# Two heads' recurrent state in fixed block-diagonal tiles: a decoder step's delta-rule scan on one core

## The chip, the cores and the metric

The kernel runs on one core of a Trainium2 chip, as one program. The metric is the device time of an execution in microseconds; a time is given as the median of several runs. A core has a matrix engine (TensorE; PE in the profile, with PEld for its loads of the stationary operand), a vector engine (VectorE, DVE), a scalar engine (ScalarE, ACT), GpSimd (POOL), and queues for transfers (here all issued by SP). Each engine works through its own instructions in order; semaphores join them. Products land in PSUM, from which DVE and ACT read.

## The reference

One step of a decoder layer over 1024 prompt tokens and 8 samples of 8 tokens: a Mamba-2 branch, an RWKV-7 branch, a merge and a gated convolutional feed-forward part. The change lies in the RWKV-7 branch alone, whose core is a recurrence over time for each of 16 heads with a state S of 64 x 64:

```python
def step(S, inp):
    r_t, w_t, k_t, v_t, kk_t, a_t = inp
    sa = jnp.einsum('bhvk,bhk->bhv', S, -kk_t)
    S = (S * w_t[:, :, None, :] + sa[..., None] * (kk_t * a_t)[:, :, None, :]
         + v_t[..., None] * k_t[:, :, None, :])
    return S, jnp.einsum('bhvk,bhk->bhv', S, r_t)
```

The prompt starts with S = 0; the samples start with given states. Decay, keys, rates and gates come from projections of the normalized input, and a group norm, a bonus and a gate follow. All results are fp32.

## The kernel before

The kernel keeps activations with channels on the 128 partitions and tokens along the free dimension, in three groups of tokens, `tg` = 0, 1, 2, with 384, 384 and 320 tokens (the last 64 are the samples'). Dense products are made with an fp32r value split in a high and a low part, three products for each (`mm3`, L254 to L257), from weights split on the way (`split_w`, L237 and L238).

The recurrence runs by chunks. Two heads share the partitions: one pair `p` of eight has head 0 on partitions 0 to 63 and head 1 on 64 to 127. A chunk, or unit `u`, is 64 steps; `tg` 0 and 1 have six units of the prompt, `tg` 2 four of them and one unit for the samples. For each pair and token group four jobs follow one another: `rw_prep` (decays, keys, masks, L486), `rw_inv` (inverse of the unit's triangular system, L601), `rw_scan` (the sequential part, L752) and `rw_post` (norm and gate, L865). Each is a generator in a lane of its own; `run_dense` takes a step of each lane (`bg.step()`) after every second inner block of six dense products, so that these small jobs stand between the dense products in PE's queue. The final order of the instructions on an engine is settled at build time by the framework's scheduler, from its planned costs and from which operands are ready; it need not be the order in which the program issues them. In the first third of the kernel all this runs; the Mamba-2 branch, the merge and the feed-forward part follow.

`rw_scan` goes like this for each unit. The state `st` is a tile of 128 x 128 in a rotating pool of eight buffers; head 0 occupies its upper left quadrant, head 1 its lower right one. L771 multiplies it with the unit's keys `ar[:, u, 0:2]` (128x128), DVE adds `rv` (L773), L775 multiplies with the inverse, DVE and ACT copy the two diagonal quadrants to `sav` (L776, L777), L779 multiplies with the decayed keys, and L781 makes the next state from all 128 x 128 elements: the old one times the unit's decay `wend`, plus the product in PSUM. The off-diagonal quadrants of the state are not used; what they give in L771 falls out later, as the quadrants of `tt` beside the diagonal are zero.

After the units of a token group come their outputs in `py` (L785 to L792), as two terms: the state at the start of the unit times the unit's `ar[:, u, 2]` (`own`), and `sav` times a masked product `tt`. Both are made by quadrant: `own` has a 64x64 stationary operand for each head, the other term a 128x64 one. `small` (L241) makes them follow one another in PE's queue, after the last product of the units. ACT and DVE then split `py` in a high and a low part (`halves`, L397) for the group norm's products.

For `tg` 0 a fresh state is filled with zeros by POOL (L758); after `tg` 2 the two quadrants of the last state are stored.

Of the kernel before, what the change touches and what calls it, by code (L numbers as in the profile page):

```python
# [10 lines left out]
F32 = mybir.dt.float32  # L11
F32R = mybir.dt.float32r
AF = mybir.ActivationFunctionType
ALU = mybir.AluOpType
# [90 lines left out]
def tile_hybrid_step(  # L105
# [6 lines left out]
    V, S, G, PE = nc.vector, nc.scalar, nc.gpsimd, nc.tensor  # L112
# [16 lines left out]
    def pst(shape=(128, 512)):  # L129
        return pp.tile(list(shape), F32, tag="t", name="pst", bufs=PB[1])  # L130
# [21 lines left out]
    def cv(name):  # L152
        o, w = CON[name]
        return con[:, o:o + w]
# [86 lines left out]
    def small(calls, behind=None, wait=None):  # L241

        for call in calls:
            if behind is None:
                behind = call().ins
            else:
                with tc.issue_after(behind):
                    behind = call().ins
            if wait is not None:
                tc.add_manual_dep(behind, wait.name, mybir.DependencyInfo(mybir.DependencyClass.Sync, mybir.DependencyReason.DATA), reason="small")  # L250
                wait = None
# [47 lines left out]
    def store(dst, src):  # L299
        nc.sync.dma_start(dst, src)  # L300
# [3 lines left out]
    rp = rw_stack.enter_context(tc.tile_pool(name="rp", bufs=1))  # L304
# [14 lines left out]
    for t in ars:  # L319
        G.memset(t[64:128, :, 0, :], 0.0)  # L320
        G.memset(t[0:64, :, 1, :], 0.0)

    llo = rp.tile([128, 2, 128], F32R, name="llo")
    G.memset(llo[64:128, 0, :].bitcast(F32), 0.0)
# [2 lines left out]
    def rt(shape, tag, bufs=1, dt=F32):  # L327
        return rp.tile(list(shape), dt, tag=tag, name=tag, bufs=bufs)
# [58 lines left out]
    start = Background({"norm": first})  # L387
# [9 lines left out]
    def halves(src, n):  # L397

        xh, xl = rt([128, 384], "xh", dt=F32R), rt([128, 384], "xl", dt=F32R)
        S.copy(xh[:, :n], src[:, :n])  # L400
        V.tensor_tensor(out=xl[:, :n], in0=src[:, :n], in1=xh[:, :n].bitcast(F32), op=ALU.subtract)
        return xh, xl
# [349 lines left out]
    def rw_scan(p, tg):  # L752
        t0, n = TG[tg]
        npu = 6 if tg < 2 else 4
        ar, tt, sav, bkt, wend, rv = jobs.pop((p, tg))
        if tg == 0:
            st = rt([128, 128], "st", 8)
            G.memset(st, 0.0)  # L758
            state[p] = st
        if tg == 2:  # L760
            s0 = rt([128, 8, 64], "s0", 1)
            nc.sync.dma_start(s0, rw0[p])
        yt = rt([128, 384], "yt", 2)

        two = lambda t: t.rearrange("p (h c) -> p h c", h=2)
        sts = []
        for u in range(npu):
            st = state[p]
            sts.append(st)
            pc = pp.tile([128, 3, 128], F32, tag="c", name="pc", bufs=2)  # L770
            PE.matmul(pc[:, 0, :], ar[:, u, 0:2, :].rearrange("p h c -> p (h c)"), st, start=True, stop=True)  # L771
            rh = rt([128, 128], "rh", 2)
            V.tensor_tensor(out=two(rh), in0=two(pc[:, 0, :]), in1=rv[:, u, :].unsqueeze(1).to_broadcast([128, 2, 64]), op=ALU.add)  # L773
            yield
            PE.matmul(pc[:, 1, :], tt[:, u, 0:2, :].rearrange("p h c -> p (h c)"), rh, start=True, stop=True)  # L775
            V.tensor_copy(sav[0:64, u, 0, :], pc[0:64, 1, 0:64])  # L776
            S.copy(sav[64:128, u, 1, :], pc[64:128, 1, 64:128])  # L777
            yield
            last = PE.matmul(pc[:, 2, :], bkt[:, u, :], sav[:, u, :, :].rearrange("p h c -> p (h c)"), start=True, stop=True).ins  # L779
            st2 = rt([128, 128], "st", 8)  # L780
            V.scalar_tensor_tensor(out=st2, in0=st, scalar=wend[:, u:u + 1], in1=pc[:, 2, :], op0=ALU.mult, op1=ALU.add)  # L781
            state[p] = st2
            yield

        py = pp.tile([128, 384], F32, tag="y", name="py", bufs=1)  # L785

        def out(u, hf, own):
            r = slice(64 * hf, 64 * hf + 64)
            lhs, rhs = (sts[u][r, r], ar[r, u, 2, :]) if own else (sav[:, u, hf, :], tt[:, u, 2 + hf, :])
            return PE.matmul(py[r, 64 * u:64 * u + 64], lhs, rhs, start=own and u == 0, stop=not own and u == npu - 1, skip_group_check=True)  # L790

        small([lambda u=u, hf=hf, own=own: out(u, hf, own) for own in (True, False) for u in range(npu) for hf in range(2)], last)  # L792
        del sts
        yield
        if tg == 2:
            S.copy(yt[:, :npu * 64], py[:, :npu * 64])
            for r in (slice(0, 64), slice(64, 128)):
                store(rw_p_o[p][r], state[p][r, r])
            u = 4
            pq = pp.tile([128, 128], F32, tag="c", name="pq", bufs=2)  # L800
            pqv = pq.rearrange("p (x b c) -> p x b c", x=2, c=8)
            arv = ar[:, 4, :, :].rearrange("p x (b c) -> p x b c", c=8)

            def sample(b, hf):
                r0, r1 = 64 * hf, 64 * hf + 64
                return PE.matmul(pqv[r0:r1, :, b, :], s0[r0:r1, b, :], arv[r0:r1, hf:3:2 - hf, b, :], start=True, stop=True)

            small([lambda b=b, hf=hf: sample(b, hf) for b in range(8) for hf in range(2)])
            qt = rt([128, 128], "qt")
            S.copy(qt, pq)  # L810
            yield
            pc = pp.tile([128, 3, 64], F32, tag="c", name="pc", bufs=2)
            for hf in range(2):
                r0, r1 = 64 * hf, 64 * hf + 64
                PE.matmul(pc[r0:r1, 0, :], qt[r0:r1, 0:64], ident[r0:r1, r0:r1], start=True, stop=True)
            rh = rt([128, 128], "rh", 2)[:, 0:64]
            V.tensor_tensor(out=rh, in0=pc[:, 0, :], in1=rv[:, u, :], op=ALU.add)
            yield
            for hf in range(2):
                r0, r1 = 64 * hf, 64 * hf + 64  # L820
                PE.matmul(pc[r0:r1, 1, :], tt[r0:r1, u, hf, 0:64], rh[r0:r1, :], start=True, stop=True)
            V.tensor_copy(sav[0:64, u, 0, :], pc[0:64, 1, :])
            S.copy(sav[64:128, u, 1, :], pc[64:128, 1, :])
            yield
            for hf in range(2):
                r0, r1 = 64 * hf, 64 * hf + 64
                PE.matmul(py[r0:r1, 256:320], sav[:, u, hf, :], tt[:, u, 2 + hf, :], start=True, stop=True)
            V.tensor_tensor(out=yt[:, 256:320], in0=py[:, 256:320], in1=qt[:, 64:128], op=ALU.add)
            pn = pp.tile([128, 512], F32, tag="c", name="pn", bufs=2)
            quarters = [(hf, b) for hf in range(2) for b in (0, 4)]  # L830
            masked = []

            def mask_quarter():
                hf, b = quarters[len(masked)]
                masked.append(rt([128, 4, 64], "sx", 2))
                G.tensor_tensor(
                    out=masked[-1], in0=sav[:, u, hf, :].unsqueeze(1).to_broadcast([128, 4, 64]),
                    in1=cv("bm")[:, b:b + 4].unsqueeze(2).to_broadcast([128, 4, 64]), op=ALU.mult,
                )

            mask_quarter()
            mask_quarter()
            yield SXP
            for q, (hf, b) in enumerate(quarters):
                PE.matmul(
                    pn[64 * hf:64 * hf + 64, 64 * b:64 * b + 256], bkt[:, u, 64 * hf:64 * hf + 64],
                    masked[q].rearrange("p b c -> p (b c)"), start=True, stop=True,
                )
                if q < 2:
                    mask_quarter()  # L850
                if q == 1:
                    yield SXP
            G.tensor_tensor(out=s0, in0=s0, in1=wend[:, 8:16].unsqueeze(2).to_broadcast([128, 8, 64]), op=ALU.mult)
            yield
            V.tensor_tensor(out=s0, in0=s0, in1=pn.rearrange("p (b c) -> p b c", c=64), op=ALU.add)
            store(rw_s_o[p], s0)
            parts_ = halves(yt, n)
        else:
            parts_ = halves(py, n)
        ps = pst()  # L860
        colsum(ps, cen_r, parts_, n)
        S.copy(yt[:, :n], ps[:, :n])
        lanes["post"].add(rw_post(p, tg, yt), lambda: (p, tg) in bonus)
# [842 lines left out]
```

## Time and profile before

| | |
|---|---|
| three runs | 2945.96, 2943.21, 2938.46 us; median 2943.21 |
| the profiled execution | 2947.11 us; span of its trace 2945.2 us |
| mean granted TensorE clock | 0.988 |
| instructions | 57204 |

The span reaches from the first to the last instruction in the trace; the execution's time holds some 1.9 us more. Times in the trace are microseconds from the span's start, and the length of an instruction is in microseconds or, where marked, nanoseconds. The ends of PE's instructions are modelled, so how long PE takes for a series is read from start to start. Neighbouring instructions of DVE may overlap a little in the same way. A busy share is a mean over stages with different limits; the scan lies between 60 and 1060 us.

### The profile page before, as it was taken

The numbers are of one execution on the slowest core, as the hardware profiler recorded it, in microseconds if no ns is written. First come the engines' busy times: TensorE is split into PE (matmuls) and PEld (weight loads), VectorE is DVE, ScalarE is ACT, GpSimd is POOL, SyncE is SP. The second block draws the span as 40 slices with busy tenths as digits, with TensorE's granted clock in tenths as the row PEclk, the third lists the DMA queues.
The fourth block names the chain that finished last, engine by engine and source line by source line (L and its number), as shares of the span: only waits on it lengthen the run. The fifth ranks groups of instructions, "written<-read, shape, count | busy, mean of one in ns | idle before, by whom it ended". The sixth has DMA issues, their size and how long they took to land.

```text
span 2945.2 us, 57204 instructions
## 1 busy us (share of the span) xinstructions
PE 2834.9 (96%) x22822; PEld 2631.3 (89%) x22822; DVE 1878.3 (64%) x4097; ACT 1365.3 (46%) x3108; POOL 698.6 (24%) x890
## 2 busy tenths in 40 slices
PE   8999999999999999999999989999999999999998
PEld 7887888888878899888888889999999999999998
DVE  6788777787788755878787753544264444444435
ACT  6666556555566655666666641222242222222223
POOL 3112212122121133555554421542220000000001
PEclk9999999999999999999999999999999999999999
DMA  3111111111111232343434564432211111111112
GB/s 113 37 36 43 42 39 51 35 47 41 45 37 41 69 86 66 115 139 111 141 108 148 150 216 128 149 110 85 83 54 51 58 51 51 51 52 57 51 51 86
DMA packets 160355, 229.86 MB, mean 78 GB/s; under 512 B 20940, under 2 KB 124632, under 8 KB 160088
## 3 DMA queue, kind: packets, MB, share of 16 engines
q1 hardware_dynamic: 160088, 226.20, 24.3%
q8 instruction: 180, 2.95, 0.4%
q14 instruction: 87, 0.71, 0.1%
HBM read 177.89 MB, written 48.26 MB: 77 GB/s over the span
## 4 chain that ended last, share of the span: by engine, by line
PE 46%; DVE 8%; ACT 4%; DMA 2%; issue 2%; POOL 1%; DVEq 0%; SPq 0%; ACTq 0%; POOLq 0%
PE psd L255 14%; PE psd L256 14%; PE psd L257 14%; DVE acc L1050 2%; DVE sg L1137 1%; DVE wlo L238 1%; DMA ld<-ya_d 1%; DVE sg L1127 1%; DVE yj L1234 1%; PE py L1180 1%; DMA ld<-yb_d 1%; DVE yj L1237 1%; PE py L1217 1%; PE py L1181 0%; PE ph L1183 0%
## 5 line engine op out<-in xcount | busy, mean ns | idle before, releaser
L255 PE MATMUL psd<-act,whi 128*128 128x384 f32 (+1 forms) x4344 | 1474.5, 339 | 14.7 <-ACT act L215 5.2
L257 PE MATMUL psd<-act,wlo 128*128 128x384 f32 (+1 forms) x4344 | 1435.0, 330 | 4.7 <-DVE wlo L238 4.7
L256 PE MATMUL psd<-act,whi 128*128 128x384 f32 (+1 forms) x4344 | 1434.2, 330 | 4.3 <-DVE act L216 4.0
L255 PEld LDWEIGHTS psd<-act,whi 128*128 128x128 f32 x4344 | 822.6, 189 | 43.9 <-issue 19.3
L256 PEld LDWEIGHTS psd<-act,whi 128*128 128x128 f32 x4344 | 822.3, 189 | 22.1 <-issue 10.0
L257 PEld LDWEIGHTS psd<-act,wlo 128*128 128x128 f32 x4344 | 822.0, 189 | 7.9 <-DVE wlo L238 5.3
L237 ACT CAST whi<-wraw 128x512 fp32r<-128x512 f32 x382 | 226.6, 619 | 499.3 <-PE psd L256 491.4
L238 DVE TENSOR_TENSOR wlo<-wraw,whi 128x512 fp32r<-128x512 f32 x382 | 289.0, 780 | 260.7 <-ACT whi L237 255.0
L1442 DVE TENSOR_TENSOR macc<-macc,psd 128x384 f32<-128x384 f32 (+1 forms) x216 | 114.6, 531 | 74.2 <-PE psd L257 73.8
L1399 POOL COPY fpo<-fraw 128x2 f32<-128x2 f32 x22 | 9.5, 430 | 613.1 <-ACT fraw L1397 613.1
L1050 DVE SCALAR_TENSOR_TENSOR acc<-craw,par,acc 128x1112 f32<-128x1112 f32 x72 | 116.3, 1615 | 5.5 <-ACT acc L1047 4.8
L1138 POOL TENSOR_TENSOR csb<-csb,cc 128x512 f32<-128x512 f32 (+1 forms) x72 | 98.5, 1374 | 77.4 <-ACT dec L1136 64.0
L1394 ACT COPY fraw<-psd 128x384 f32<-128x384 f32 x44 | 21.1, 479 | 133.2 <-PE psd L257 133.2
L1304 POOL TENSOR_TENSOR ld<-ld,rw 128x384 f32<-128x384 f32 (+1 forms) x48 | 54.3, 1152 | 114.7 <-DMA ld<-ya_d 111.0
L1326 POOL TENSOR_TENSOR macc<-macc,gt 128x384 f32<-128x384 f32 (+1 forms) x48 | 53.6, 1118 | 107.1 <-DVE gt L1325 107.1
L546 POOL TENSOR_TENSOR ar<-rm,wq 128x384 f32<-128x384 f32 (+1 forms) x24 | 20.8, 867 | 237.9 <-ACT wq L524 221.1
L1325 DVE TENSOR_TENSOR gt<-psd,gt 128x384 f32<-128x384 f32 (+1 forms) x48 | 25.5, 533 | 77.9 <-PE psd L257 70.7
L713 POOL MEMSET tt<- 64x384 f32 (+1 forms) x48 | 18.1, 377 | 240.6 <-PE pst L697 239.1
L1137 DVE TENSOR_TENSOR sg<-sg,cbm 128x512 f32<-128x512 f32 (+1 forms) x72 | 73.5, 1045 | 0.6
L613 ACT COPY uc<-tt 32x192 f32<-32x192 f32 (+1 forms) x96 | 49.4, 515 | 52.5 <-DVE tt L581 51.3
L627 POOL TENSOR_TENSOR bk<-bk,wend 128x768 f32<-128x768 f32 (+1 forms) x24 | 34.2, 1426 | 140.7 <-PE pst L573 104.8
L779 PE MATMUL pc<-sav,bkt 128*128 128x128 f32 x256 | 59.3, 314 | 8.3 <-ACT sav L777 7.0
(405 smaller groups left out, 4360.8 us busy)
## 6 DMA issues: line engine op xcount, KB each, us to landing
wraw<-in_wts SPq DMA_DIRECT2D x191, 512.0 KB, 3.2
csb<-cs_d SPq DMA_DIRECT2D x64, 256.0 KB, 4.2
gt<-g_d SPq DMA_DIRECT2D x48, 192.0 KB, 2.3
zt<-z_d SPq DMA_DIRECT2D x32, 256.0 KB, 4.6
z_d<-ge SPq DMA_DIRECT2D x32, 192.0 KB, 1.9
ya_d<-yj SPq DMA_DIRECT2D x8, 768.0 KB, 4.4
ld<-ya_d SPq DMA_DIRECT2D x32, 192.0 KB, 3.2
g_d<-ge SPq DMA_DIRECT2D x28, 192.0 KB, 1.9
```

Source lines behind the costliest of these rows:

```text
L237: S.copy(hi[:, c:c + 512], t[:, c:c + 512])
L238: V.tensor_tensor(out=lo[:, c:c + 512], in0=t[:, c:c + 512], in1=hi[:, c:c + 512].bitcast(F32), op=ALU.subtract)
L255: PE.matmul(ps, a, act[:, 0, :n], start=first, stop=False)
L256: PE.matmul(ps, a, act[:, 1, :n], start=False, stop=False)
L257: PE.matmul(ps, b, act[:, 0, :n], start=False, stop=last)
L779: last = PE.matmul(pc[:, 2, :], bkt[:, u, :], sav[:, u, :, :].rearrange("p h c -> p (h c)"), start=True, stop=True).ins
L1050: V.scalar_tensor_tensor(out=acc, in0=raw[:, j:j + L], scalar=cw(j), in1=acc, op0=ALU.mult, op1=ALU.add)
L1137: V.tensor_tensor(out=sg[0:m, :, :m], in0=sg[0:m, :, :m], in1=cbm[0:m, :m].unsqueeze(1).to_broadcast([m, 4, m]), op=ALU.mult)
L1138: G.tensor_tensor(out=ec[:, :, :m], in0=ec[:, :, :m], in1=cx[:, q0:q0 + m].unsqueeze(1).to_broadcast([128, 4, m]), op=ALU.mult)
L1304: G.tensor_tensor(out=t[:, :n], in0=t[:, :n], in1=scales[k // 4, tg][:, :n], op=ALU.mult)
L1326: G.tensor_tensor(out=macc[m][tg][:, :n], in0=macc[m][tg][:, :n], in1=gt[:, :n], op=ALU.add)
L1442: V.tensor_tensor(out=x1[m][tg][:, :n], in0=x1[m][tg][:, :n], in1=ps[:, :n], op=ALU.add)
```

## The change

The states get eight fixed tiles `st0` to `st7`, filled with zeros once at the start and used in turn; a state's update writes only the two quadrants on the diagonal, with one instruction for each head, so the quadrants beside it stay zero. A fresh state for `tg` 0 has only its two diagonal quadrants filled. Since the whole tile is now block-diagonal, `own` is one 128x128 product for both heads in place of two 64x64 ones. The second term is as before.

```diff
+    diag = [rp.tile([128, 128], F32, name=f"st{i}") for i in range(8)]
+    for t in diag:
+        G.memset(t, 0.0)
+    turn = [0]
+
+    def next_state():
+        turn[0] += 1
+        return diag[turn[0] % 8]
...
         if tg == 0:
-            st = rt([128, 128], "st", 8)
-            G.memset(st, 0.0)
+            st = next_state()
+            for r in (slice(0, 64), slice(64, 128)):
+                G.memset(st[r, r], 0.0)
             state[p] = st
...
-            st2 = rt([128, 128], "st", 8)
-            V.scalar_tensor_tensor(out=st2, in0=st, scalar=wend[:, u:u + 1], in1=pc[:, 2, :], op0=ALU.mult, op1=ALU.add)
+            st2 = next_state()
+            for r in (slice(0, 64), slice(64, 128)):
+                V.scalar_tensor_tensor(out=st2[r, r], in0=st[r, r], scalar=wend[r, u:u + 1], in1=pc[r, 2, r], op0=ALU.mult, op1=ALU.add)
...
-        def out(u, hf, own):
+        def own(u):
+            return PE.matmul(py[:, 64 * u:64 * u + 64], sts[u], ar[:, u, 2, :], start=u == 0, stop=False, skip_group_check=True)
+
+        def out(u, hf):
             r = slice(64 * hf, 64 * hf + 64)
-            lhs, rhs = (sts[u][r, r], ar[r, u, 2, :]) if own else (sav[:, u, hf, :], tt[:, u, 2 + hf, :])
-            return PE.matmul(py[r, 64 * u:64 * u + 64], lhs, rhs, start=own and u == 0, stop=not own and u == npu - 1, skip_group_check=True)
-
-        small([lambda u=u, hf=hf, own=own: out(u, hf, own) for own in (True, False) for u in range(npu) for hf in range(2)], last)
+            return PE.matmul(py[r, 64 * u:64 * u + 64], sav[:, u, hf, :], tt[:, u, 2 + hf, :], start=False, stop=u == npu - 1, skip_group_check=True)
+
+        small([lambda u=u: own(u) for u in range(npu)] + [lambda u=u, hf=hf: out(u, hf) for u in range(npu) for hf in range(2)], last)
```

## Rows read from the trace of the kernel before

**Rows 1.** The page's first part, the whole span: for each engine its busy us, its share of the span and its instructions.

```profile
PE 2834.9 (96%) x22822; PEld 2631.3 (89%) x22822; DVE 1878.3 (64%) x4097; ACT 1365.3 (46%) x3108; POOL 698.6 (24%) x890
```

**Rows 2.** The table by stretches, 60 to 1060 us, core 0. Columns: the stretch, its length, busy us (and instructions) of PE, PEld, DVE, ACT and POOL, the granted TensorE clock as a share of full speed, the DMA engines' share, GB/s. The last row sums all six stretches of the answer.

```profile
200.00:400.00 200.00, 189.40 (x2200) 159.72 (x2199) 159.03 (x473) 123.10 (x315) 41.85 (x76) 1.00 0.14 48
...
sum 1000.00, PE 955.30 PEld 817.08 DVE 766.21 ACT 606.61 POOL 176.93; mean PE 159.22 PEld 136.18 DVE 127.70 ACT 101.10 POOL 29.49
```

**Rows 3.** PE's instructions in order of time, at the end of a scan with six units and at the end of one with four (from 168 and from 1049 us). Columns: start in us, us from the first start to the last end, engine, line, operation, tiles, size of the stationary operand, size of the moving one, how many in a row. A product of fp32 is two records, one a pass.

```profile
168.58 0.92 PE L790 MATMUL py<-ar,st 64*64 64x64 f32 x24
169.43 0.92 PE L790 MATMUL py<-tt,sav 128*64 128x64 f32 x24
...
1049.96 0.68 PE L790 MATMUL py<-ar,st 64*64 64x64 f32 x16
1050.58 0.69 PE L790 MATMUL py<-tt,sav 128*64 128x64 f32 x16
```

**Rows 4.** The same view around 1047 us: a run of products on 64x64 quadrants with 16 columns streamed, and what follows it.

```profile
1047.30 1.11 PE L806 MATMUL pq<-ar,s 64*64 64x16 f32 x32
1048.34 0.49 PE L775 MATMUL pc<-rh,tt 128*128 128x128 f32 x2
```

**Rows 5.** All instructions that touch the tile `st`, and what they waited for. Columns of the first three: how many records, ns least/median/most of one, first and last start in us, forms. The last one: us in total and times that an engine stood idle until that instruction ended (here until L781, ahead of L771).

```profile
L790 PE MATMUL py<-ar,st x512: 216/218/267, 168.6 to 1050.4; 64*64 64x64 f32 x171
...
L771 PE MATMUL pc<-st,ar x256: 270/275/378, 115.7 to 1047.1; 128*128 128x128 f32 x128
L781 DVE SCALAR_TENSOR_TENSOR st<-st,wend,pc x128: 302/346/350, 136.7 to 1050.1; 128x128 f32<-128x128 f32 x128
...
  DVE st L781: 11.0, 27
```

**Rows 6.** PE's instructions in order of time around 572 us: three transposes in a row and the next instruction.

```profile
572.45 0.49 PE L638 MATMUL pst<-con,vm 128*128 128x128 f32 x3
572.77 0.39 PE L771 MATMUL pc<-st,ar 128*128 128x128 f32 x2
```

**Rows 7.** DVE's instructions in order of time, around one state update (168 to 169 us).

```profile
167.99 0.26 DVE L424 SCALAR_TENSOR_TENSOR km<-psd,par,km 128x56 f32<-128x56 f32 x1
168.17 0.16 DVE L663 TENSOR_REDUCE zl<-pd 128x5 f32<-128x25 f32 x1
...
168.69 0.35 DVE L781 SCALAR_TENSOR_TENSOR st<-st,wend,pc 128x128 f32<-128x128 f32 x1
168.95 0.22 DVE L659 TENSOR_TENSOR pd<-zl,vt 128x36 f32<-128x36 f32 x1
...
169.18 0.68 DVE L238 TENSOR_TENSOR wlo<-wraw,whi 128x512 fp32r<-128x512 f32 x1
```

**Rows 8.** The same view at two places where lines that work on one half of the partitions follow each other: L553 for the lower half (147.40) and the upper (149.34); L556 and L557 for the lower half (195.77, 196.25), then for the upper (196.81, 197.28).

```profile
147.40 0.23 DVE L553 TENSOR_TENSOR ar<-k,wq 64x64 f32<-64x64 f32 x1
147.53 0.69 DVE L679 TENSOR_REDUCE zl<-pd 128x64 f32<-128x512 f32 x1
...
148.96 0.35 DVE L681 TENSOR_SCALAR ub<-zl,con 128x256 f32<-128x256 f32 x1
149.34 0.22 DVE L553 TENSOR_TENSOR ar<-k,wq 64x64 f32<-64x64 f32 x1
149.59 0.71 DVE L683 STREAM_TRANSPOSE pd<-ub 128x512 f32<-128x512 f32 x1
...
195.77 0.55 DVE L556 SCALAR_TENSOR_TENSOR bk<-a,sg 64x384 f32<-64x384 f32 x1
196.25 0.54 DVE L557 TENSOR_TENSOR bk<-c,sg 64x384 f32<-64x384 f32 x1
196.81 0.56 DVE L556 SCALAR_TENSOR_TENSOR bk<-a,sg 64x384 f32<-64x384 f32 x1
197.28 0.55 DVE L557 TENSOR_TENSOR bk<-c,sg 64x384 f32<-64x384 f32 x1
197.87 0.35 DVE L781 SCALAR_TENSOR_TENSOR st<-st,wend,pc 128x128 f32<-128x128 f32 x1
```

**Rows 9.** Who waited for whom between 60 and 1056 us. Columns: the waiting instruction, the one that it waited for, us in total, times, longest us.

```profile
DVE sav L776 <- PE pc L775: 39.9, 56, 2.1
...
DVE st L781 <- PE pc L779: 26.9, 30, 1.7
...
PEld pc L779 <- ACT sav L777: 24.1, 60, 1.5
...
DVE rh L773 <- PE pc L771: 16.9, 25, 1.4
...
PEld pc L775 <- DVE rh L773: 12.3, 32, 1.2
...
PE pc L779 <- ACT sav L777: 7.0, 15, 1.2
...
PE pc L775 <- DVE rh L773: 3.3, 8, 0.9
```

**Rows 10.** POOL's instructions in order of time at the start; in brackets the idle time ahead of one and what ended it.

```profile
3.86 0.20 POOL L758 MEMSET st<- 128x128 f32 x1
11.64 0.85 POOL L367 TENSOR_TENSOR a<-tt 128x384 f32<-128x384 f32 x1 [7.59 <-DMA tt<-in_xt]
```

## The prediction

> **What bounds the kernel now.** I read the page's busy times first, then a table of the stage that the change touches, then the bare order of instructions inside one group of the scan, then who waits for the scan's tiles. The page gives PE 96% of the span and DVE 64% [rows 1]. [...] So in that stage TensorE is the bound with DVE as its nearest rival, 44.7 us of PE's time is visibly idle, and what is added to PE's queue is paid nearly in full, while what is added to DVE is paid only where PE comes to wait for it. The other two thirds of the kernel use nothing that the change touches.
>
> **PE: the outputs' first term.** Before, a unit of 64 steps takes two 64x64 products, one on either quadrant of the diagonal, each in two passes. The order of instructions shows the group of 24 such passes starting at 168.58 and the next group at 169.43: 0.85 us. A group of 16 takes 0.62 us (1049.96 to 1050.58) [rows 3]. Two quadrants run side by side, so these are 12 and 8 rounds: the difference, 0.23 us over 4 rounds, is 0.058 us a round, and 0.85 - 12 x 0.058 = 0.15 us stands for entering the 64x64 form behind another one. The streamed width does not set the round: L806, with 16 columns streamed in place of 64, needs 1.04 us for 16 rounds, which is (1.04 - 0.15) / 16 = 0.056 [rows 4]. The loading of the stationary 64 columns sets it. The same shows in the first pass of a group, where the load isn't covered: 267 ns at most against 218 for L790 (49 more), but 378 against 275 for the 128x128 form of L771 (103 more) [rows 5]. A load of 128 columns takes twice as long as one of 64.
>
> After, a unit takes one 128x128 product of 64 columns, two passes, each with a load of 128 columns. No row has that form. The nearest is L638, 128x128 with 128 columns streamed: three passes from 572.45 to 572.77, 0.107 each [rows 6]. Load and stream may both be that long there; with 64 columns streamed the load remains. I take 0.107. Bounds: from below 0.058 a pass (only the stream counts, and the new pass costs what a round cost); from above 0.107 + 0.053 = 0.160 (load and stream add up, a stream of 64 columns being half of one of 128).
>
> A group of six units goes from 12 rounds of 0.058 to 12 passes of 0.107, +0.59 us, and one change of form (0.15 us) falls away, because the product before it (L779, or a dense one) is 128x128 too: +0.44. A group of four units: 8 x 0.049 - 0.15 = +0.24. There are 8 pairs of heads with two groups of six and one of four: 16 x 0.44 + 8 x 0.24 = **+9.0 us**; by the lower bound 24 x -0.15 = -3.6 us, by the upper 16 x 1.07 + 8 x 0.67 = +22 us. Nothing hides it but PE's idle 4.5%, so I give nothing back.
>
> [...]
>
> **DVE: the state in two halves.** L781 is one instruction of 128 columns: 0.35 us long, and the next one starts 0.26 us after it, since DVE lets neighbours overlap. L424, the same operation from PSUM with 56 columns, takes 0.26 and lets the next start after 0.18 [rows 7]. Between these, 64 columns give 0.27 long and 0.19 to the next. But the second half lies on partitions 64 to 127, and the rows on L556 and L557 show what such a switch does: two instructions on the lower half follow at 0.48 us, lower to upper at 0.56, and upper to the next instruction from partition 0 at 0.59: the overlap is lost at both switches, 0.08 and 0.11 us. L553, with 64 columns, shows it in small: on the lower half the next starts 0.13 us after it, on the upper half 0.25 [rows 8]. So the pair occupies DVE for 0.19 + 0.08 + 0.19 + 0.11 = 0.57 us instead of 0.26, **+0.31 us a unit and 40 us over 128 units**, and the state is complete 0.27 + 0.27 = 0.54 us after the start instead of 0.35: +0.19.
>
> [...]
>
> What of the 40 us reaches PE? The next L771 waits for the state, and PE's queue is in order, so the dense products behind it wait too. It waited 27 times of 128 [rows 5]: 27 x 0.19 = 5 us at least, 128 x 0.19 = 24 us if every unit did. The remaining DVE queue (L773's sum, L776's copy, the weight splits of L238) moves back by 0.31 us until DVE next runs dry. PE waited 40 times of 128 for L773, and 75 times for L777, which follows L776; but DVE had run dry before 25 of the L773, 56 of the L776 and 30 of the L781 [rows 9]. I put this at a fifth of 40 us, 8 us, between nothing and 40. Sum for DVE: **+13 us**, with 5 and 40 as its ends. One thing could make it dearer: the order on an engine isn't the program's (between L557 and L781 in rows 8 stand lanes of different jobs), so a long instruction may get between the two halves, and then the state is late by that one's length, such as L238's 0.68 us [rows 7].
>
> **POOL, and what costs nothing.** The eight new 128x128 fills at the start come at 0.20 us each, 1.6 us, before POOL's first wait for an input: POOL is idle from 4.06 to 11.64 us [rows 10]. That wait for the DMA hides them; without it they would cost 1.6 us. The fill for a new pair of heads becomes two of 64x64 in place of one of 0.20 us [rows 10]: POOL is busy 177 of 1000 us in the stage, and this idle time hides the second fill; without it, 8 x 0.20 = 1.6 us. Fixed tiles in turns of eight give the same reuse distance as the pool's eight buffers. No DMA is added or moved; SP's queue stays as it is.
>
> **Sum.** The profiled execution took 2947.1 us, its span 2945.2 and 1.9 around it. 2947.1 + 9 + 13 = 2969 us on its own footing. It lies 3.9 us above the median of the three runs shown (2943.2), so the median after should be near **2965 us**, 0.7% slower. A measurement of this kernel can tell about 0.3% (8.8 us) from no change.
>
> **Rivals.**
> (a) DVE becomes the pace of the scan: its chain has no slack left and the full 0.31 us of every unit is paid. 9 + 40 = 49 us, 2992. For it: 766 us of DVE in 1000 become 806. Against: the chain of a unit takes about 7 us of the stage's time (128 units between 136.7 and 1050.1 us [rows 5]), far above its three products and three DVE steps. Chance 0.12.
> (b) DVE's share is covered, and PE's idle time takes up part of the product's: with a few us of DVE's, +5 to +12 us, 2948 to 2955. For it: 101 of 128 L771 didn't wait. Against: the 40 and 75 waits of L775 and L779. Chance 0.15.
> (c) The other side, not slower: a full pass of 64 columns costs what a round of two quadrants did, because loads of 128 columns hide. -3.6 us, with DVE covered as in (b): 2940. It decides from a pass of 0.058 + 0.15/12 = 0.071 us downward, where the first term gets no dearer. For it: no row has the form. Against: 103 ns of load in L771. Chance 0.06.
> (d) The two halves overlap on DVE after all: 2 x 0.19 - 0.26 = 0.12 us a unit, 15 us of DVE time instead of 40, of which 27 x 0.12 + 0.2 x 15 = 6.2 us is paid; 2943 + 9 + 6.2 = 2958. Chance 0.08.
> (e) The instructions' order on the engines is settled when the program is built, and other durations and tiles can shift it. PE's 44.7 idle us are what it can play with; to be faster by 0.3% it would have to take back the sum and 8.8 us, some 31 of these. Chance 0.05, of which 0.04 is faster.
>
> **How the numbers follow.** My forecast, slower with both terms, holds 0.54, its own range 2955 to 2982. The range for all reaches from (b) to (a), 2946 to 2994; (c) and most of (e) are left out. Slower by over 0.3%: 0.54 + 0.12 + 0.08 and 0.06 of (b) = 0.80. Within 0.3%: (c), 0.09 of (b), 0.01 of (e) = 0.16. Faster: 0.04.
>
> **What would show it.** In the profile after: 256 passes of the first term where 512 were, in groups of 12 that take 1.28 us (8: 0.86), with no gap ahead of them; if a group takes 0.7, (c) is right. Two L781-like halves of some 0.27 us, the second starting only when the first has ended; if it starts after 0.19, (d). L771's waits for the state up from 11 us towards 20 or more; unchanged, (b); near 128 waits, (a). PE's busy time in the stage up by about 9 us and its idle time by about 13. The stages behind the scan should keep their lengths; if they don't, (e). I would be wrong above all through DVE's share, the only term that isn't read from a row but guessed between two.

## The result and the profile after

Four executions of the changed kernel gave a median of 2984.97 us (2977.41 to 2989.26), the kernel before beside it 2944.59 (2938.46 to 2947.22): a ratio of 1.0134 [1.0119, 1.0148], 40 us slower. The forecast was 2965 with a range of 2946 to 2994. The direction and the range held; of the 40 us, 22 had been forecast.

The first part of the page, which answers to [rows 1], is of the execution that took 2989.26 us (span 2987.3): for each engine its busy us, its share of the span and its instructions.

```profile
PE 2864.9 (96%) x22566; PEld 2653.8 (89%) x22566; DVE 1914.9 (64%) x4225; ACT 1367.5 (46%) x3108; POOL 704.5 (24%) x906
```

There are 256 fewer PE instructions, 128 more on DVE, 16 more on POOL: the change did what the diff says. DVE is busy 36.6 us longer, PE 30.0.

The lines have moved by 10 or 11: L782 is the product with the state (L771 before), L784 the sum `rh` (L773), L786 the product with the inverse (L775), L787 and L788 the copies to `sav` (L776, L777), L790 the product with the decayed keys (L779), L793 the state's halves (L781), L800 `own`, L804 the second term. First PE's order at the end of a scan with six units and of one with four, as in [rows 3].

```profile
172.34 0.39 PE L790 MATMUL pc<-sav,bkt 128*128 128x128 f32 x2
172.56 1.45 PE L800 MATMUL py<-ar,st 128*128 128x64 f32 x12
173.94 0.74 PE L804 MATMUL py<-tt,sav 128*64 128x64 f32 x18
...
1098.28 0.38 PE L790 MATMUL pc<-sav,bkt 128*128 128x128 f32 x2
1098.49 1.00 PE L800 MATMUL py<-ar,st 128*128 128x64 f32 x8
1099.43 0.69 PE L804 MATMUL py<-tt,sav 128*64 128x64 f32 x16
```

(The first of these views ends at 174.5 us and cuts its last group short.) The twelve passes take 1.38 us from start to start where the 24 took 0.85, the eight 0.94 where the 16 took 0.62. Nothing stands idle ahead of them. By these groups the term is 16 x 0.53 + 8 x 0.32 = 11.0 us.

Then DVE around one update of the state, as in [rows 7].

```profile
172.64 0.18 DVE L673 TENSOR_REDUCE zl<-pd 128x6 f32<-128x36 f32 x1
172.76 0.57 DVE L793 SCALAR_TENSOR_TENSOR st<-st,wend,pc 64x64 f32<-64x64 f32 x2
173.37 0.19 DVE L673 TENSOR_REDUCE zl<-pd 128x6 f32<-128x36 f32 x1
```

From the first half to the next instruction of another line it is 0.61 us; it was 0.26. So a unit takes 0.35 us more of DVE, 45 us over 128 units.

Last, the tile `st`, as in [rows 5]: records, ns least/median/most, first and last start, forms; below, the us and times that an engine stood idle until that instruction ended, and then the us and times that the named one waited for a user of `st`.

```profile
L782 PE MATMUL pc<-st,ar x256: 270/275/583, 116.7 to 1095.7; 128*128 128x128 f32 x128
L793 DVE SCALAR_TENSOR_TENSOR st<-st,wend,pc x256: 227/281/291, 138.8 to 1099.0; 64x64 f32<-64x64 f32 x128
...
L800 PE MATMUL py<-ar,st x256: 217/275/474, 172.6 to 1099.2; 128*128 128x64 f32 x128
...
  DVE st L793: 10.9, 26
...
  POOL st L769: 33.2, 6
```

Two things are to be seen. The last update starts at 1099.0 where it was 1050.1: the stage of the scan has lost 48.9 us. And PE waits for the state no more than before: 10.9 us, 26 times, against 11.0 and 27. The 33.2 us that POOL's fill now waits for an old reader of its tile is new.

To see where the stage loses, I followed the dense products: the k-th one (L255) starts later than its counterpart of before by 2.3 us at k = 200, 10.4 at 400, 16.1 at 600, 21.9 at 800, 33.1 at 900, 47.3 at 1000, 48.8 at 1100 (the end of the scan) and 41.9 at the last. That is a drift of some 22 us, and then two jumps. The table by stretches (columns as in [rows 2]) shows what lies at the jumps:

```profile
400.00:600.00 200.00, 190.66 (x1954) 160.74 (x1948) 159.66 (x494) 119.42 (x305) 34.56 (x64) 1.00 0.11 38
...
800.00:1000.00 200.00, 189.55 (x2027) 159.57 (x2026) 151.73 (x448) 113.23 (x290) 34.44 (x65) 0.92 0.10 35
1000.00:1060.00 60.00, 55.97 (x545) 47.51 (x545) 48.21 (x155) 35.10 (x89) 9.47 (x19) 0.94 0.17 59
```

The granted clock is 1.00 in the first of these and 0.92 and 0.94 in the others. In the execution profiled before, the trace has no moment below full clock between 40 and 1210 us. So there are three suspects: the own product, the pair of halves, and TensorE's clock.

### The profile page after: what moved, and what is told of

Its sections match the earlier page's. It is cut to its first block, busy times and chain, and to the rows that moved or that the text cites. A ratio compares the mean times of both kernels' runs of the same rounds, so it can differ in the third digit from the quotient of the medians.

```text
span 2987.3 us, 56835 instructions
## 1 busy us (share of the span) xinstructions
PE 2864.9 (96%) x22566; PEld 2653.8 (89%) x22566; DVE 1914.9 (64%) x4225; ACT 1367.5 (46%) x3108; POOL 704.5 (24%) x906
## 3 DMA queue, kind: packets, MB, share of 16 engines
q1 hardware_dynamic: 160088, 226.20, 23.6%
## 4 chain that ended last, share of the span: by engine, by line
PE 42%; DVE 8%; ACT 5%; DMA 2%; issue 2%; POOL 2%; DVEq 0%; SPq 0%; ACTq 0%; POOLq 0%
PE psd L255 13%; PE psd L256 13%; PE psd L257 13%; DVE acc L1064 2%; DVE sg L1151 1%; DVE wlo L238 1%; DVE yj L1248 1%; DVE sg L1141 1%; DMA ld<-yb_d 1%; DMA ld<-ya_d 1%; DVE act L216 1%; DVE yj L1251 1%; ACT csb L1146 0%; ACT sg L1144 0%; ACT whi L237 0%
## 5 line engine op out<-in xcount | busy, mean ns | idle before, releaser
L255 PE MATMUL psd<-act,whi 128*128 128x384 f32 (+1 forms) x4344 | 1472.5, 339 | 15.6 <-ACT gt L441 4.7
L255 PEld LDWEIGHTS psd<-act,whi 128*128 128x128 f32 x4344 | 822.7, 189 | 44.9 <-issue 19.8
L793 DVE SCALAR_TENSOR_TENSOR st<-st,wend,pc 64x64 f32<-64x64 f32 x256 | 70.9, 277 | 29.8 <-PE pc L790 25.5
L556 POOL TENSOR_TENSOR ar<-rm,wq 128x384 f32<-128x384 f32 (+1 forms) x24 | 21.2, 884 | 232.6 <-ACT wq L534 211.8
L790 PE MATMUL pc<-sav,bkt 128*128 128x128 f32 x256 | 60.2, 317 | 10.5 <-ACT sav L788 8.2
L790 PEld LDWEIGHTS pc<-sav,bkt 128*128 128x128 f32 x256 | 40.2, 191 | 32.4 <-ACT sav L788 28.0
```

The lines of the kernel that those rows point to most:

```text
L255: PE.matmul(ps, a, act[:, 0, :n], start=first, stop=False)
L793: V.scalar_tensor_tensor(out=st2[r, r], in0=st[r, r], scalar=wend[r, u:u + 1], in1=pc[r, 2, r], op0=ALU.mult, op1=ALU.add)
```

## The experiments

The first four kernels each hold one part of the change; they ran on one chip, beside 15 executions of the kernel before (median 2944.42). Losses in us are worked out from the ratio.

**Fixed tiles alone.** The changed kernel with one update of 128 columns and `own` by quadrants, as before.

```diff
-            for r in (slice(0, 64), slice(64, 128)):
-                V.scalar_tensor_tensor(out=st2[r, r], in0=st[r, r], scalar=wend[r, u:u + 1], in1=pc[r, 2, r], ...)
+            V.scalar_tensor_tensor(out=st2, in0=st, scalar=wend[:, u:u + 1], in1=pc[:, 2, :], ...)
```

> The kernel before with the eight fixed tiles in turn and their fills, but with the state's update in one instruction of 128x128 and the first term in two quadrants. Its instructions stand on PE, DVE and ACT in the order of the kernel before; on POOL the fills move. If only the two priced terms (the full product and the two halves) count: no change, within 5 us of before. If the fixed tiles or the moved fills (POOL waits for them 33 us in the kernel after) are part of the loss: 5 to 20 us slower.

Measured: 2945.91 us, ratio 1.0003 [0.9992, 1.0015]. Fixed tiles in turn, the fills at the start and two fills for a fresh state cost nothing that can be measured (-2 to +4 us). What POOL waits for in this kernel is nearly the same as in the changed one, so that wait is harmless:

```profile
  POOL st L769: 29.6, 6
```

**The full product alone.** The kernel before, with `own` as one 128x128 product. The state's quadrants beside the diagonal aren't zero here, so the two heads are mixed in the first term.

```diff
+        def own(u):
+            return PE.matmul(py[:, 64 * u:64 * u + 64], sts[u], ar[:, u, 2, :], start=u == 0, ...)
```

> The kernel before (pool of eight buffers, update in one instruction), with the first term as one 128x128 product for a pair. The quadrants beside the diagonal aren't zero here, so the outputs' first term mixes the two heads: it is a kernel for its time alone. By the prediction's first term: +9 us, and nothing on DVE. If the loss of 40 us comes from the product (it delays what stands behind it, or moves the order), +20 us or more.

Measured: 2954.25 us, ratio 1.0033 [1.002, 1.0046]: +9.8 us, with 5.9 to 13.5 as the interval's ends.

**The halves alone.** The changed kernel with `own` by quadrants as before.

> The kernel after with the first term in two quadrants again: fixed tiles and the update in two halves alone. By the prediction's second term: +13 us (5 to 40). If the measured 40 us is the two terms and DVE's was too small: about +30. If the two only cost together: under +10.

Measured: 2969.96 us, ratio 1.0083 [1.0068, 1.0098]: +24.5 us. The pair is the larger part of the loss, nearly twice the 13 us forecast for it. It doesn't come alone, though: the scheduler settles another order for it. Of the 4097 instructions on DVE in the kernel before, some 3770 keep their relative order, and of 3105 on ACT some 2920; with the fixed tiles alone all of them do. The 24.5 us are the price of the pair together with this order.

**The same without the change of partitions.** As the halves alone, but each instruction updates 64 columns on all 128 partitions. The instructions stand in the same order on DVE, ACT and POOL in both kernels, and on PE but for a few records of 20 thousand, so that the two differ in how long DVE takes.

```diff
-            for r in (slice(0, 64), slice(64, 128)):
-                V.scalar_tensor_tensor(out=st2[r, r], in0=st[r, r], scalar=wend[r, u:u + 1], in1=pc[r, 2, r], ...)
+            for c in (slice(0, 64), slice(64, 128)):
+                V.scalar_tensor_tensor(out=st2[:, c], in0=st[:, c], scalar=wend[:, u:u + 1], in1=pc[:, 2, c], ...)
```

> As halves_only, but the two instructions take 64 columns each on all 128 partitions, so that both start at partition 0; the instructions stand in the same order on every engine. If the lost overlap at the switch of partitions carries the cost: DVE occupied 0.38 us a unit in place of 0.61, and some half of what halves_only loses comes back. If it is the second instruction as such, or the order that it brings: the same time as halves_only within 3 us.

Measured: 2960.63 us, ratio 1.005 [1.0034, 1.0066]: +14.8 us. DVE in order of time at the same update, first with the halves alone, then by columns:

```profile
172.83 0.58 DVE L793 SCALAR_TENSOR_TENSOR st<-st,wend,pc 64x64 f32<-64x64 f32 x2
173.43 0.19 DVE L673 TENSOR_REDUCE zl<-pd 128x6 f32<-128x36 f32 x1
```

```profile
172.45 0.47 DVE L793 SCALAR_TENSOR_TENSOR st<-st,wend,pc 128x64 f32<-128x64 f32 x2
172.84 0.18 DVE L673 TENSOR_REDUCE zl<-pd 128x6 f32<-128x36 f32 x1
```

The pair occupies 0.60 us in one and 0.39 in the other. The difference, 0.21 us, is the lost overlap at the two switches of partitions: 27 us over 128 units, of which 9, a third, reach the end. It was forecast as 0.08 + 0.11 = 0.19.

Who waits for whom between 60 and 1100 us with the halves alone (columns as in [rows 9]):

```profile
DVE sav L787 <- PE pc L786: 37.8, 42, 2.2
...
DVE st L793 <- PE pc L790: 25.4, 25, 1.7
...
PEld pc L786 <- DVE rh L784: 17.4, 36, 1.3
...
DVE rh L784 <- PE pc L782: 15.3, 32, 1.3
...
PEld pc L782 <- DVE st L793: 9.0, 20, 0.7
...
PE pc L786 <- DVE rh L784: 8.5, 16, 1.0
...
PE pc L782 <- DVE st L793: 2.7, 9, 0.4
```

The wait for the state is 11.7 us in 29 times, as good as before. The wait for `rh` is 25.9 us in 52 times; in [rows 9] it was 12.3 + 3.3 = 15.6 in 40. Summed over all rows of the table, PE's and PEld's waits for DVE rise from 47.7 to 68.3 us, by 21 of the 25 lost. By columns this sum is 48.9, though: there the 15 us don't show as waits for DVE. From that kernel to the halves the sum rises by 19.4 us and the time by 9.3, so a sum of waits is not a loss.

By columns the waits for ACT and POOL are 2.8 and 4.5 us longer, and part of this stands in one place. Followed by its dense products, this kernel's scan loses 4.8 of the 12.2 us by which it ends late within one step, between 240 and 256 us of the kernel before; the halves lose 4.9 there. PE stands idle ahead of two products of the samples (in brackets how long and what ended it; first the kernel before, which has no wait there, then by columns), and from 247.9 us the granted clock is at half, 0.5 of full speed, for 3.4 us:

```profile
237.34 0.34 PE L827 MATMUL py<-tt,sav 128*64 128x64 f32 x4
...
241.31 1.08 PE L845 MATMUL pn<-sx,bkt 128*64 128x256 f32 x4
```

```profile
244.52 0.33 PE L839 MATMUL py<-tt,sav 128*64 128x64 f32 x2 [0.70 <-ACT sav L835]
...
247.24 0.65 PE L857 MATMUL pn<-sx,bkt 128*64 128x256 f32 x2 [1.76 <-POOL sx L848]
```

Between the two groups 24 dense products stand on PE in the kernel before, and three by columns; and on POOL `bk` and `um`, 4.2 us of work, come ahead of `sx` and no longer behind it. So this wait comes from the new order, not from the time that the two instructions take on DVE.

**The queue without the lateness.** The fixed tiles alone, and behind each update an instruction of the upper half's size that writes a spare tile. Nobody waits for it, so the state is as early as before, and only what stands behind it on DVE is late.

```diff
             V.scalar_tensor_tensor(out=st2, in0=st, ...)
+            r = slice(64, 128)
+            V.scalar_tensor_tensor(out=spare[r, r], in0=st[r, r], scalar=wend[r, u:u + 1], in1=pc[r, 2, r], ...)
```

> tiles_only with one instruction more on DVE behind each state update: the upper half's update once more, into a spare tile that nobody reads. The state itself is complete as early as in the kernel before; DVE is occupied some 0.4 us a unit longer, 50 us in all, a little more than by the two halves (45). If what is paid is the queue behind the update (other work of DVE comes late), +20 to +30 us. If it is the state's own lateness that PE waits for, within +5.

Measured on another chip, like the three kernels after it, beside seven executions of the kernel before (median 2944.73): 2964.3 us, ratio 1.0068 [1.0047, 1.0088], +20 us. DVE at one update:

```profile
172.74 0.33 DVE L793 SCALAR_TENSOR_TENSOR st<-st,wend,pc 128x128 f32<-128x128 f32 x1
173.10 0.29 DVE L795 SCALAR_TENSOR_TENSOR spare<-st,wend,pc 64x64 f32<-64x64 f32 x1
173.42 0.21 DVE L670 TENSOR_TENSOR pd<-zl,vt 128x25 f32<-128x25 f32 x1
```

The two occupy 0.68 us, 0.42 more than the one of before, 54 us in all, and 20 are paid with the state on time. So a loss nearly as large as that of the halves needs no late state; the forecast had given the queue 8. But the order of the instructions is neither that of the kernel before (some 3740 of 4097 on DVE keep their relative order) nor that of the halves, so the 20 us are the queue and a new order together, and the two costs can't be subtracted.

**DVE's time as a currency.** If DVE's time in the scan has a price, relief should pay. The kernel before, with the bonus's product (L540) on POOL and its scale applied where it is split, so that DVE should have some 12 us less to do.

```diff
-        V.scalar_tensor_tensor(out=rn[:, :n], in0=rr[:, :n], scalar=pv("rk", p), in1=k2[:, :n], ...)
+        G.tensor_tensor(out=rn[:, :n], in0=rr[:, :n], in1=k2[:, :n], op=ALU.mult)
```

> The kernel before with one of its DVE instructions (L540, 0.53 us to the next, 24 times, 12 us in all) made on POOL, its scale by channel being applied in the split that follows. If DVE's occupied time is what the scan pays for, at about half of it: 5 to 7 us faster. If DVE's time is covered, or POOL (about 1 us for it) makes others late: no change or slower.

Measured: 2961.29 us, ratio 1.0059 [1.0036, 1.0082]: 17 us slower, a clear miss. DVE got no relief, either:

```profile
PE 2835.1 (96%) x22822; PEld 2632.5 (89%) x22822; DVE 1886.7 (64%) x4073; ACT 1368.2 (46%) x3108; POOL 725.4 (25%) x914
```

It has 24 instructions fewer and is busy 8.4 us longer than in [rows 1]: the 13.7 us of L540 are gone, but others take longer, `ar` (L553) 31.8 us in place of 24.2. The order of instructions on DVE changed as well (some 3710 of 4073 keep their relative order). So this experiment says nothing of the price of DVE's time; whether the new order costs the 17 us, or POOL's product that comes too late for its reader, isn't shown.

**Do the parts add up?** The changed kernel by columns and with the full product; the order on every engine is that of the changed kernel. (The quadrants beside the diagonal aren't zero here, and the heads are mixed in the first term, in all three runs of this kernel.)

> The kernel after with the update in two instructions of 64 columns on all partitions, so that no switch of partitions falls between them. Its instructions stand in the order of the kernel after. The quadrants beside the diagonal aren't zero then, so the outputs' first term mixes the two heads: for its time alone. If the parts add up: 9.8 + 14.8, about +25 us. If the order of the kernel after costs something of its own (that kernel is 40 us slower, its parts 34.5): +30 or more.

Measured: executions of 2967.06, 2984.7, 2985.03 and 2985.62 us; ratio of the medians 1.0123 [1.0088, 1.0157]. Their mean granted clocks are 0.988, 0.982, 0.983 and 0.980. At 0.988 the time as a whole is additive (2944.7 + 9.8 + 14.8 = 2969); with the lower clock it isn't. One program, one order of instructions, two times: the clock was suspected.

**The changed kernel again.**

> The kernel after once more, for a second profile and an interval beside the others. If the low clock around 860 and 980 us belongs to this order of instructions, it is there again; if it was one execution's, the stage ends some 15 us earlier in the trace and the time is about +35.

Measured: 2984.6 us (2974.14 to 2987.36), ratio 1.0125 [1.0094, 1.0155]. The fall of the clock near 860 us isn't there in this profile; the one near 970 to 1000 is. The median is that of the kernel by columns (2984.87): in this order the 9 us between halves and columns don't show in the medians. They show at like clocks: the executions of the changed kernel with 0.988 took 2974.14, 2977.41 and 2982.67 us, the one by columns 2967.06.

**Three more profiles.** One execution each, on the first of the two chips, beside one of the kernel before (2949.78 us).

> The kernel of after_by_columns once more (the heads are mixed in the first term, as there), for one profile. Its four executions lay at 2967 (granted clock 0.988) and at 2985 (0.980 to 0.983), and only the first was profiled. If what separates them is TensorE's clock falling to half near 970 to 1000 us, as in the kernel after: an execution near 2985 shows 13 us or more at half clock between 950 and 1010 us, and its last L793 some 10 us or more later than the 1077 us or so of the profiled one; one near 2967 shows 8 us or less there. If the difference comes from elsewhere (transfers, the later stages): the scan ends at the same time in both, and the clock there is 1.00 in both.

> As columns_second_look, a further execution: by the clock theory its time goes with the time at half clock in 60 to 1100 us, about half a microsecond for each microsecond at half clock; by the rival it doesn't.

> The changed kernel once more, for one profile. Two profiled executions (2987 and 2989 us) show about 20 us at half clock between 960 and 1010 us. By the clock theory an execution at 2986 or more shows these again, and one at 2975 to 2980 shows 10 us or more fewer at half clock over the whole span. By the rival, that the clock is the same in both and other waits differ, the time at half clock is the same within 5 us.

For each profiled execution I summed the time that the trace shows at half clock, and took by how much the 1100th dense product, at the end of the scan, starts later than before:

| execution | us | at half clock, 60 to 1105 us | at half clock, later | end of the scan later by |
|---|---|---|---|---|
| before | 2947.11 | 0 | 64 | |
| fixed tiles | 2945.88 | 3 | 64 | 1.8 |
| full product | 2957.33 | 3 | 53 | 9.8 |
| halves | 2972.55 | 10 | 57 | 23.6 |
| by columns | 2963.18 | 7 | 63 | 12.2 |
| changed kernel | 2989.26 | 48 | 43 | 48.8 |
| the same, again | 2987.36 | 27 | 61 | 39.5 |
| the same, third profile | 2985.82 | 7 | 75 | 34.1 |
| changed, by columns | 2967.06 | 14 | 47 | 27.4 |
| the same, second profile | 2970.14 | 14 | 54 | 27.1 |
| the same, third profile | 2980.14 | 31 | 55 | 33.9 |
| extra instruction behind | 2964.02 | 14 | 53 | 20.0 |
| bonus on POOL | 2959.10 | 10 | 46 | 16.3 |

The third profile of the changed kernel, with little low clock in the scan, ends it 34.1 us late: 9.8 for the full product and 23.6 for the halves make 33.4. By columns the sum falls short: 9.8 and 12.2 make 22.0, and two profiles with 14 us of low clock end the scan 27.1 and 27.4 us late. So the parts add up in one case and miss 5 us in the other. Between executions of one program the end of the scan goes with the clock: 14.7 us for 41 us more at half clock, 0.36 us for each; in the kernel by columns 6.8 us for 17, 0.40; but the second profile of the changed kernel, set against its third, has 5.4 us for 20.5, 0.26. The half microsecond expected was too much. Two points went against the expectations. In the third profile by columns most of the low clock came at 853 us, 17.1 us of it, and only 3.4 near 990. And the third profile of the changed kernel took 2985.82 us although the scan went well, since the stages behind it had 75 us at the lower level and gave 4 us more away.

The order of the changed kernel has something of its own as well. In all six profiles of it, halves or columns, the clock falls at least once between 967 and 1001 us, for 3.4 to 20.5 us in all; in no profile of the other kernels is there a fall in that stretch. Here is PE in the third profile of the changed kernel:

```profile
969.95 0.49 PE L790 MATMUL pc<-sav,bkt 128*128 128x128 f32 x2 [1.80 <-ACT sav L788]
...
985.65 0.33 PE L841 MATMUL py<-tt,sav 128*64 128x64 f32 x2 [0.70 <-ACT sav L837]
988.06 1.22 PE L859 MATMUL pn<-sx,bkt 128*64 128x256 f32 x4 [2.09 <-POOL sx L850]
```

Neither the halves alone nor the full product alone has these three waits there. Between 936 and 959 us of the kernel before, where this place lies, the scan falls 6.8 us further behind, and 989.7 us is where its clock falls.

The same stretches of two executions of the one program show how sudden this is (columns as in [rows 2]); first the changed kernel as profiled at first, then its third profile:

```profile
850.00:860.00 10.00, 9.45 (x199) 8.14 (x198) 9.10 (x22) 5.39 (x15) 1.79 (x5) 1.00 0.06 21
860.00:870.00 10.00, 10.00 (x106) 8.02 (x107) 4.11 (x9) 2.16 (x6) 0.23 (x1) 0.54 0.24 74
870.00:880.00 10.00, 10.00 (x54) 7.90 (x54) 4.63 (x13) 3.39 (x8) 5.15 (x7) 0.61 0.01 2
```

```profile
850.00:860.00 10.00, 9.45 (x210) 7.56 (x208) 8.28 (x22) 6.94 (x20) 2.02 (x5) 1.00 0.05 18
860.00:870.00 10.00, 10.00 (x130) 8.24 (x131) 5.86 (x14) 3.95 (x10) 4.59 (x6) 1.00 0.20 59
870.00:880.00 10.00, 9.03 (x49) 6.74 (x48) 9.92 (x41) 4.11 (x11) 2.03 (x4) 1.00 0.13 43
```

PE works through much the same instructions in both, busy 9.45 us of 10 ahead of the fall. In one execution the clock falls to half at 860 us, in the other it doesn't.

## Why the prediction was right or wrong

**The first term: right.** +9.0 forecast, +9.8 measured. A pass takes 0.111 to 0.112 us where 0.107 was taken from the transposes, which stream 128 columns [rows 6], and a group 1.38 and 0.94 where 1.28 and 0.86 were forecast. A pass that streams 64 columns is no shorter than one of 128, and twice as long as a round of 64x64 products (0.058): in these rows the spacing goes with the stationary columns, as the prediction had it. The records of the loads alone differ by less, 192 ns in the median for `own` after against 135 before. Rival (c), that loads of 128 columns hide, is out.

**Fixed tiles and fills: right at nothing.** The tiles alone give a ratio of 1.0003. The cover named for POOL holds even with 33.2 us of new waiting there.

**DVE's occupancy: right within a tenth.** 0.57 us a pair forecast, 0.61 measured; 45 us instead of 40. The second half doesn't overlap the first (with the halves alone 0.58 us for the two, a median of 0.285 for one), which rules out (d); at the update shown, the two columns' instructions, which stay on all partitions, do overlap (0.47 for the two, 0.27 for one). The 9.3 us between the medians of these two kernels, one order of instructions, are the price of the overlap that the halves lose.

**What of it reaches PE: this step failed.** The prediction put 5 us on the wait for the state and "a fifth of 40 us" on the queue, 13 in all; the halves alone cost 24.5. The first part didn't show where it was said to: that wait stayed at 11 us. (By the prediction's own sign that spoke for (b), which the time rules out.) For the rest the runs leave two readings open. Either the fifth was too small, and 0.54 of the pair's 45 us is paid. Or the price was about right, and the new order costs the rest, which the prediction knew as rival (e) and put at nothing in its sum. For the second speak the two kernels of one order, where 27 us of DVE's time cost 9.3. At that price, an estimate, the pair's 45 us come to 15 and the 17 us of the columns to 6, and some 9 us are left in both kernels, of which the step near 250 us is in part a wait for POOL and ACT. Against it: the first 17 us of DVE's time need not cost what the next 27 do. No run has the pair in the order of the kernel before. The argument for the fifth was that DVE had run dry before many of the steps that PE waits for [rows 9]. That count hardly moved, from 111 to 99 (32 before `rh`, 42 before `sav`, 25 before `st`), while `rh` made PE wait 52 times instead of 40: it doesn't tell the loss. Rival (a), the full price of all 128 units, asked 40 us of the halves alone and is out as well. So is (b), in which PE's idle time covers nearly all of it.

**The clock: not priced.** The forecast's 44.7 idle us of PE are what the sum of [rows 2] leaves of 1000, and it has no term for a clock below the 1.00 shown there. The part effects make 34.3 us; the measured loss is 40. Of the 41.9 us by which the last dense product of the first profile is late, 34.1 is the stage with little of the low clock, 14.7 what the low clock took there, and 6.9 came back behind the scan, where this execution had 43 us at half clock and that of before 64 (21 x 0.36 = 7.6). From execution to execution this varies: nine of the changed kernel lie between 2974 and 2989 us. At a like clock the loss is smaller. The three executions at 0.988 have a mean of 2978.1 us; four of the kernel before at 0.988 (2943.95, 2946.55, 2947.11 and 2947.58) have 2946.3. That is 32 us, so some 8 of the 40 go with the clock.

**The later stages** keep their lengths within 7 us, mostly in step with the clock; by columns they give 4.0 us more away at nearly the same time at half clock (63 and 64 us). Rival (e), the order of instructions, isn't out. It was thought of as a gain or a loss by itself; the waits at 247 and 970 to 988 us come with the order, and the sum of the parts can't test it, since the halves already hold a new order.

**The range held in part by luck.** Its upper end, 2994, came from rival (a), whose full price isn't paid. What filled it was 11.5 us more for the halves than forecast, whatever their share of order, and the low clock, which no term had.

**What stays open.** How the 24.5 us divide between DVE's time and the order. Why the clock falls in some executions and not in others: several falls in the scan (near 123, 248 and 990 us) come within some 3 us of a place where PE stood idle for 1.8 to 2.2 us, but the kernel before has such a place at 122.6 us, 2.17 us long, without a fall, and ahead of the fall at 860 us PE was busy. Whether another order would avoid the waits and the falls wasn't tried. None of these kernels is faster than the one before.

## What to carry to other kernels

Splitting a small vector instruction in two by partitions cost more here than a second instruction does by itself (at one update 0.60 us for the two halves, 0.39 for two instructions on all partitions, 0.26 for the one of before): read the start-to-start time over a switch of partitions from the trace and multiply it by the number of units. How much of it is paid at the end is less certain: here, in a stage where the second engine is busy three quarters of the time, a third was paid where the order stayed the same and a half together with a new order, whoever waits for the instruction itself. Don't take a count of "ran dry" as cover. Check whether an experiment keeps the order of instructions before calling its loss the price of an engine's time. And before explaining the last few microseconds of a difference by the code, compare two or three profiles of the same kernel side by side with the granted clock.

## What the runs showed of the hardware

TensorE's granted clock fell from full speed to half (1.00 to 0.5) in the midst of work, in one case with PE busy 9.45 us of the 10 ahead of it, stayed there for 3.4 to 17.1 us, and came back; the place differs between executions of one program, though six profiles of one order all have a fall between 967 and 1001 us. A microsecond more at half clock went with 0.26 to 0.40 us more in the scan, in three pairs of executions of one program. And the two switches of partitions between neighbouring DVE instructions together cost 0.21 us a pair (0.60 against 0.39 us at the update shown), though both halves have half the elements of the instructions by columns.
